# A hybrid decoder block on one Trainium2 core: the recurrence's gates from one operand of high and low rows, both gates in its columns

## The chip, the core and the metric

The kernel runs on one core of a Trainium2 chip. The time is device microseconds of an execution, and the number to compare is the median of three runs. Everything is float32 outside; inside, products on TensorE take operands of type fp32r, and each float32 operand is split into a high part (what fp32r keeps) and a low part (the rest), so that one exact product becomes three: high by high, low by high, high by low.

## The reference

The block is one layer with 512 positions and a width of 1024:

- `h = RMSNorm(x)`, `z = h @ W_in`, whose columns feed three mixers and their gates: a gated MLP with a causal matrix over chunks of 128, sparse attention (compressed, selected and window branches), and a recurrent block.
- `x = x + RMSNorm(W_o(sum of sigmoid(gate) * (branch @ W_br)))`, then `x = x + RMSNorm(SwiGLU(RMSNorm(x)))`.

The change is in the recurrent block. It has 16 heads of 64 channels:

```python
xc = causal depthwise convolution of width 4 over xr, plus conv_b
xh = xc.reshape(B, S, RNN_HEADS, RNN_HEAD_DIM)
r = sigmoid(einsum('bshi,hio->bsho', xh, w_a) + b_a)      # one 64x64 matrix per head
i = sigmoid(einsum('bshi,hio->bsho', xh, w_x) + b_x)      # another one per head
a = exp(-8 * r * softplus(-lam))
h_t = a_t * h_{t-1} + sqrt(1 - a_t**2) * (i * xc)_t
```

and its output is `h * gelu(gate)`.

## The kernel before, in words

**Layout.** Channels lie on the 128 partitions and the 512 positions along the free dimension, so a tile of 128 x 512 holds two heads of the recurrence. A product of a 128-column weight tile with a 128 x 512 operand fills one PSUM bank. A matrix of 1024 input channels takes 8 x 3 = 24 such products (function `passes`, line 259). There are eight banks: six with the tag `mm`, two with the tag `tr` in this phase.

**Stages.** First come the value half of the gated MLP (`v_half`, line 614, 96 products for each of its two halves, into four banks each, by chunk of 128 positions) and one tile for the compressed attention; then the eight tiles of the recurrence (`xr_tile`), in two batches of four, with the eight gelu tiles of its gate (`rg_tile`) and the attention's compression (`compress`, line 771) among and behind them; then the branch products, the attention, the output projection and the feed-forward network.

**A tile of the recurrence** (`xr_tile`, lines 476 to 506). 24 products give the tile; ScalarE takes it out of PSUM with scale and bias (line 488), VectorE adds the three shifted terms of the convolution (line 490). ScalarE copies the high part `ch`, VectorE subtracts for the low part `cl` (`split`, lines 131 and 136). For each of the two gates, three products (line 498) of a 128 x 128 weight tile, which has the two heads' 64 x 64 matrices on its diagonal and zeros beside them, go into a bank `tr`: high weights by `ch`, high weights by `cl`, low weights by `ch`. Sigmoid (line 500) and Tanh (line 503, the second sigmoid as `(1 + tanh)/2`) take the banks out, and one step of VectorE (line 504) multiplies by the convolved input. `yield 4` says that the gates are issued four steps after the split, behind the next tile's products.

**Behind a batch** (`rec_batch`): Tanh on each tile, one Sqrt over the four, Exp on each, two steps of VectorE and the scan per tile. Sqrt and Exp each load a table on ScalarE.

**The gate weights** (`load_wab`, lines 453 to 463). One DMA from SP (line 455) brings the array `wab`, 128 x (2 gates x 8 tiles x 128 columns), 1 MB, 8 KB per partition, with the zeros already in it. Four splits of 512 elements per partition make the high and low weights.

**Weights in general.** `unit` hands out a matrix's high and low weights; `wload` loads the raw tile (line 204; two buffers) and splits it, so that the split for the matrix after the next one is written when a matrix begins. ScalarE writes the high part, VectorE the low one.

**Start.** Eleven float32 products of ones with ones (line 349, 128 x 128 each, in one bank) run while the first loads are under way. POOL fills constants meanwhile.

**What sets the order.** The text of the kernel gives each instruction a place: `run` interleaves a main list of generators with a side list, at a given rate, and holds back a generator that yields a number. The framework then plans the order of each engine's queue from the expected times of all instructions when the kernel is built, by readiness and place in the text; `issue_after` adds a fixed order where the text wants one. On the chip every engine's queue runs strictly in the planned order. A DMA is issued by the queue of the engine named (SP, ScalarE or POOL). Tiles of one tag share their buffers in turn: the tag `row` has six, which hold `xc`, `ch`, `cl` and the gelu's temporaries; the tag `s1`, into which the raw gate weights go, has one that nothing used before.

Of the kernel before, what the change touches and what calls it, by code (L numbers as in the profile page):

```python
# [25 lines left out]
F32R = mybir.dt.float32r  # L26
I32 = mybir.dt.int32
AF = mybir.ActivationFunctionType
# [5 lines left out]
NK = 8  # L34
# [9 lines left out]
V_CW, V_CB, V_BA, V_BX, V_LAM = 48, 80, 88, 96, 104  # L44
# [8 lines left out]
def hybrid_block(ctx: ExitStack, tc: tile.TileContext, A, out):  # L53
    nc = tc.nc
    V, SC, GP, PE, SY = nc.vector, nc.scalar, nc.gpsimd, nc.tensor, nc.sync
# [42 lines left out]
    def nm(s):  # L98
        cnt[0] += 1
        return f"{s}_{cnt[0]}"  # L100

    def slab(name, dt=F32, tag=None, shape=(4, S), first=0):
        pool, bufs = (merge if tag == "m" else big, TAGS[tag]) if tag in TAGS else phase_pool[tag]
        if tag not in ("y", "mo", "f", "wab"):
            return pool.tile([128, *shape], dt, tag=tag, name=nm(name), bufs=bufs)
        size = 2064 if tag == "f" else 2112
        t = pool.tile([128, size], dt, tag=tag, name=nm(name), bufs=bufs)[:, first:first + math.prod(shape)]
        return t if len(shape) == 1 else t.rearrange(
            "p (a b) -> p a b" if len(shape) == 2 else "p (a b c) -> p a b c", **dict(zip("abc", shape)))

    def row(name, dt=F32, tag="row", first=0):
        bufs = {"row": 6, "q32": 2, "tg": 2}[tag]
        return mid.tile([128, S if tag == "row" else S + 32], dt, tag=tag, name=nm(name), bufs=bufs)[:, first:first + S]

    def bank(tag):
        return psum[1].tile([128, S], F32, tag=tag, name=nm(tag), bufs=psum[2][tag])
# [10 lines left out]
    def f32(ap):  # L127
        return ap.bitcast(F32)

    def split(src, hi, lo, lo_eng=None):  # L130
        res["hi"] = SC.activation(hi, src, AF.Copy)  # L131
        e = lo_eng or V
        if e is GP:
            GP.tensor_sub(lo, src, f32(hi))
        else:
            res["lo"] = V.tensor_sub(lo, src, f32(hi))  # L136

    res = {}
# [126 lines left out]
    def matrix(ps, xh, xl, m=128):  # L265
        hi, lo = unit()
        yield from passes(ps, hi, lo, xh, xl, m)
# [5 lines left out]
    def const0(shape, name):  # L273
        return phase_pool["s0"][0].tile(shape, F32, name=name, bufs=1)
# [7 lines left out]
    vec = const0([128, NVEC], "vec")  # L282
    SY.dma_start(vec, A["vec"])
    wload(1)
    ones = const0([128, 128], "ones")
    half = const0([128, 3, 8], "half")
# [57 lines left out]
                      start=True, stop=True)  # L344


    pw = bank("mm")
    for _ in range(11):
        PE.matmul(pw[:, :128], ones, ones, start=True, stop=True)

    gh, gl = Pair("gxh", F32R, "y"), Pair("gxl", F32R, "y")
    hh, hl = Pair("hh", F32R, "h"), Pair("hl", F32R, "h")

    def scaled(k):
# [94 lines left out]
    wab = {}  # L451

    def load_wab():
        raw = slab("wabr", tag="s1", shape=(2, NK, 128))
        SY.dma_start(raw, A["wab"])
        hi = slab("wabh", F32R, "wab", (2, NK, 128), 48)
        lo = slab("wabl", F32R, "wab", (2, NK, 128), 48)
        wab["hi"], wab["lo"] = hi, lo
        for _ in range(4):
            yield  # L460
        for k in range(0, NK, 2):
            split(raw[:, :, k:k + 2], hi[:, :, k:k + 2], lo[:, :, k:k + 2])
            yield

    yc = {}
    rec = {}
# [11 lines left out]
    def xr_tile(b, c):  # L478
        if c == 0:
            rec[b] = dict(R=slab("r", tag="y" if b else "m"), GG=slab("gg", tag="m"), TI=slab("ti", tag=("s0", "s1")[b]))  # L480
        k = 4 * b + c
        ps = bank("mm")
        yield from matrix(ps, hh, hl)
        xc = row("xc")

        def cw(w):
            return vec[:, V_CW + 8 * w + k:V_CW + 8 * w + k + 1]
        res["xc"] = SC.activation(xc, ps, AF.Identity, scale=cw(3), bias=vec[:, V_CB + k:V_CB + k + 1])
        for i in (1, 2, 3):
            res["cv"] = V.scalar_tensor_tensor(xc[:, i:], ps[:, :S - i], cw(3 - i), xc[:, i:], op0=OP.mult, op1=OP.add)  # L490
        yield
        ch, cl = row("ch", F32R), row("cl", F32R)
        split(xc, ch, cl)
        yield 4
        for g, dst in ((0, "R"), (1, "TI")):
            pg = bank("tr")
            for t, (w, x) in enumerate((("hi", ch), ("hi", cl), ("lo", ch))):
                PE.matmul(pg, wab[w][:, g, k, :], x, start=(t == 0), stop=(t == 2))  # L498
            if g == 0:
                SC.activation(rec[b]["R"][:, c, :], pg, AF.Sigmoid, bias=vec[:, V_BA + k:V_BA + k + 1])  # L500
            else:
                ti = rec[b]["TI"][:, c, :]
                last = SC.activation(ti, pg, AF.Tanh, scale=0.5, bias=half[:, 0, k:k + 1])
                res["ti"] = last, V.scalar_tensor_tensor(ti, ti, 1.0, xc, op0=OP.add, op1=OP.mult)
            yield

# [1540 lines left out]
    def xr_tiles(b, nxt):  # L2047

        tiles = four(xr_tile, b) + [nxt]
        return tiles[:1] + [behind(t, "xc", "cv") for t in tiles[1:]]  # L2050
# [4 lines left out]
    def branch(b, y, j0=0, j1=8):  # L2055
# [3 lines left out]
        return r  # L2059

    run([v_half(0), v_half(1), cmp_tile(0)], seq(norm(), load_wab()))
    run(xr_tiles(0, gate_tile()))
    tiles = xr_tiles(1, rg_tile(1, 0))
# [139 lines left out]
```

## Time and profile before

| | |
|---|---|
| median of three runs | 1093.67 us (1092.62 to 1093.85) |
| profiled execution, first to last instruction | 1090.5 us |
| mean granted clock of TensorE in it | 0.998 of full |
| TensorE busy | 1080.7 us (99%) |
| VectorE busy | 883.2 us (81%) |
| ScalarE busy | 658.9 us (60%) |
| POOL busy | 30.2 us (3%) |
| moved by DMA | 115.06 MB in 34943 packets, 3440 of them under 512 B |

The profile shows one execution. Its own total is known only as the span from the first to the last instruction; what lies around it is not in the trace. "PE" is TensorE, "PEld" its weight loads, "DVE" VectorE, "ACT" ScalarE, "SPq" and "ACTq" the queues of SP and ScalarE where they issue DMAs. A row of the timeline has the start, the duration, the engine, the line, the operation, what is written from what, the shape, how many, and in brackets the idle time before it and what ended it. A row of a group has the shortest, median and longest duration in ns, then the first and last start. A row of stretches has the stretch, its length, and for each engine the busy time and count.

### The profile page before, as it was taken

The page shows a single profiled execution, that of the slowest core. Times are in us where ns is not written, and L with a number is a line of the kernel's source. Part 1 is how long each engine was busy: PE and PEld are TensorE (multiplying, and loading weights), DVE is VectorE, ACT ScalarE, POOL GpSimd, SP SyncE. Part 2 cuts the span into 40 slices and gives each one's busy share as a digit, 9 for nine tenths or more (in the row PEclk, how much of TensorE's full clock was granted, in tenths as well). Part 3 has the DMA queues.
Part 4 walks back from the last instruction along what each step waited for, and adds up shares of the span by engine and source line. Part 5 has one row for each costly group of instructions (what it writes and reads, how often), then busy time and mean ns, then how long its engine had stood idle before and what let it go on. Part 6 is the DMA issues. An engine that isn't in the chain of part 4 may idle for free.

```text
span 1090.5 us, 16726 instructions
## 1 busy us (share of the span) xinstructions
PE 1080.7 (99%) x6440; PEld 948.2 (87%) x6440; DVE 883.2 (81%) x1552; ACT 658.9 (60%) x1207; POOL 30.2 (3%) x43
## 2 busy tenths in 40 slices
PE   9999999999999999999999999999999999999997
PEld 7888888999889888898888789988999999998885
DVE  6967779669675899998998887877987888889665
ACT  6757574454444676876777655555656665667552
POOL 1000000000000000000000000000000000022200
PEclk9999999999999999999999999999999999999999
DMA  8332325420322211102111134261323232379902
GB/s 313 104 103 84 97 85 199 182 99 20 116 78 78 78 59 39 59 20 78 59 39 59 58 119 134 76 251 39 117 78 117 100 117 94 135 213 219 185 21 96
DMA packets 34943, 115.06 MB, mean 106 GB/s; under 512 B 3440, under 2 KB 3728, under 8 KB 33968
## 3 DMA queue, kind: packets, MB, share of 16 engines
q1 hardware_dynamic: 28064, 96.93, 26.0%
q0 software_dynamic: 5216, 11.18, 5.1%
q10 hardware_dynamic: 1584, 5.90, 1.4%
q8 instruction: 50, 0.82, 0.3%
q14 instruction: 29, 0.24, 0.1%
HBM read 111.89 MB, written 2.10 MB: 105 GB/s over the span
## 4 chain that ended last, share of the span: by engine, by line
PE 96%; DVE 2%; DMA 1%; ACT 1%; issue 0%; SPq 0%; DVEq 0%; ACTq 0%
PE mm L259 37%; PE mm L1740 16%; PE mm L1876 7%; PE mm L1260 7%; PE mm L1496 4%; PE o L979 4%; PE mm L614 4%; PE sc L941 3%; PE tr L966 3%; PE tr L1876 3%; PE mm L857 2%; PE tr L771 1%; PE tr L498 1%; PE mm L1598 1%; DMA raw<-in_w_v 1%; PE tr L674 1%
## 5 line engine op out<-in xcount | busy, mean ns | idle before, releaser
L259 PE MATMUL mm<-hh,hi 128*128 128x512 f32 x504 | 199.5, 396 | 0.0
L259 PE MATMUL mm<-hh,lo 128*128 128x512 f32 x504 | 197.4, 392 | 0.0
L259 PE MATMUL mm<-hl,hi 128*128 128x512 f32 x504 | 197.0, 391 | 0.0
L136 DVE TENSOR_TENSOR lo<-raw,hi 128x1024 fp32r<-128x1024 f32 (+1 forms) x104 | 121.1, 1164 | 36.9 <-ACT hi L131 34.0
L131 ACT ACTIVATE hi<-raw 128x1024 fp32r<-128x1024 f32 (+1 forms) x104 | 105.2, 1011 | 50.3 <-PE mm L259 18.9
L259 PEld LDWEIGHTS mm<-hh,lo 128*128 128x128 f32 x504 | 94.6, 188 | 19.6
L259 PEld LDWEIGHTS mm<-hl,hi 128*128 128x128 f32 x504 | 94.7, 188 | 18.4 <-issue 0.2
L259 PEld LDWEIGHTS mm<-hh,hi 128*128 128x128 f32 x504 | 94.7, 188 | 18.1 <-PE mm L1260 0.2
L947 ACT ACTIVATE P<-P,ast 128x128 f32<-128x128 f32 (+3 forms) x128 | 70.7, 555 | 23.0 <-DVE ast L945 22.2
L945 DVE CUSTOM_DVE_ANT_0 P<-sc,mask 128x128 f32<-128x128 f32 (+3 forms) x128 | 57.9, 484 | 8.1 <-PE sc L941 7.3
L131 ACT ACTIVATE ph<-tr 128x512 fp32r<-128x512 f32 x80 | 46.9, 592 | 26.2 <-PE tr L966 23.0
L136 DVE TENSOR_TENSOR pl<-tr,ph 128x512 fp32r<-128x512 f32 x80 | 54.4, 686 | 2.9 <-ACT ph L131 0.9
L941 PE MATMUL sc<-K,q 128*128 128x512 f32 (+2 forms) x192 | 51.0, 368 | 0.0
L1740 PE MATMUL mm<-t,hi 128*128 128x256 f32 x288 | 50.7, 276 | 0.0
L1876 PE MATMUL mm<-hi,u 128*128 128x512 f32 x160 | 50.4, 390 | 0.1
L966 PE MATMUL tr<-ident,P 128*128 128x128 f32 x320 | 48.7, 273 | 0.0
L966 PEld LDWEIGHTS tr<-ident,P 128*128 128x128 f32 x320 | 39.1, 140 | 9.6 <-DVE pl L136 1.0
L136 DVE TENSOR_TENSOR lo<-bs,hi 128x1024 fp32r<-128x1024 f32 x28 | 34.1, 1222 | 13.6 <-ACT hi L131 13.5
L1740 PEld LDWEIGHTS mm<-t,hi 128*128 128x128 f32 x288 | 43.3, 188 | 0.0
L1740 PE MATMUL mm<-fh,hi 128*128 128x256 f32 x144 | 40.0, 278 | 0.0
L1740 PE MATMUL mm<-fh,lo 128*128 128x256 f32 x144 | 39.8, 276 | 0.0
L1740 PE MATMUL mm<-fl,hi 128*128 128x256 f32 x144 | 39.8, 276 | 0.0
(474 smaller groups left out, 2895.0 us busy)
## 6 DMA issues: line engine op xcount, KB each, us to landing
raw<-in_w_in SPq DMA_DIRECT2D x64, 512.0 KB, 3.5
rawp<-in_w_fi SPq DMA_DIRECT2D x20, 1024.0 KB, 4.8
bs<-in_w_fo POOLq DMA_DIRECT2D x20, 512.0 KB, 7.4
raw<-in_w_br SPq DMA_DIRECT2D x14, 512.0 KB, 3.5
w<-in_cw ACTq DMA_DIRECT2D x4, 1024.0 KB, 7.3
raw<-in_w_o SPq DMA_DIRECT2D x8, 512.0 KB, 3.9
bs<-in_w_fo SPq DMA_DIRECT2D x8, 512.0 KB, 7.9
raw<-in_w_v SPq DMA_DIRECT2D x7, 512.0 KB, 5.1
```

The costliest lines, as they stand in the source:

```text
L131: res["hi"] = SC.activation(hi, src, AF.Copy)
L136: res["lo"] = V.tensor_sub(lo, src, f32(hi))
L259: res["mm"] = PE.matmul(ps[:m, n0:n1], w[:, k * 128:k * 128 + m], x[k][:, n0:n1], start=(t == 0), stop=(t == 3 * NK - 1))
L614: res["mm"] = PE.matmul(b[c], x[k][:, c * 128:(c + 1) * 128], w[:, kk * 512:kk * 512 + 512], start=(k == 0 and t == 0), stop=(k == NK - 1 ...
L941: PE.matmul(ps[:, :w * n].rearrange("p (b n) -> p b n", b=w), lhs, K[:, i, brs[0]:brs[-1] + 1, :n], start=(i == 0), stop=(i == 1))
L945: V.tensor_tensor_reduce(out=t, in0=ps[:, b * n:b * n + n], in1=mask[0][:, S - n:], scale=-0.125, scalar=3.0e38, op0=OP.add, op1=OP.min, a ...
L947: SC.activation(t, t, AF.Exp, scale=-1.0, bias=st[:, 0, j, b:b + 1], accum_out=st[:, 1, j, b:b + 1])
L966: PE.transpose(pt[:, j * 128:(j + 1) * 128], self.part(j, br)[:, kt * 128:(kt + 1) * 128], ident)
L979: PE.matmul(po, VV[:, kt, g % 2, br].rearrange("p i d -> p (i d)"), x, start=(br == 0 and kt == 0 and t == 0), stop=(br == 1 and kt == a a ...
L1260: res["mm"] = PE.matmul(ps, u[:, k * 128:k * 128 + 128], v[:, k], start=(start and k == t == 0), stop=(k == 3 and t == 2), skip_group_chec ...
L1740: res["mm"] = PE.matmul(ps, w[:, k * 128:k * 128 + 128], x[:, k], start=(start and k == t == 0), stop=(k == 3 and t == 2), skip_group_chec ...
L1876: PE.matmul(ps, a, b, start=id(ps) not in begun, stop=i == len(ops) - 1, skip_group_check=True)
```

## The change

Per tile and head there is one operand of 128 rows: 64 rows of the head's high part in the head's own half of the partitions, and 64 rows of its low part in the other half. The weight tile for that head has the head's matrices laid twice down the rows, so that the product adds what the high and the low rows give; its first 64 columns are the first gate's matrix, its last 64 columns the second's. Two products per head (high weights, low weights) replace three per gate. The result of one head holds the first gate in the bank's lower 64 partitions and the second in the upper ones, so Sigmoid and Tanh are issued per head, on 64 partitions each, and write the head's half of the partitions. The high part is copied in two halves, and the low part is subtracted in two halves that are written across to the other half of the partitions.

The weights come in eight DMAs of 64 partitions x 8 tiles x 64 columns, four from SP and four from ScalarE, in runs of 64 elements (256 B). The splits run over the flat array, 512 elements at a time.

The warm-up has seven of the eleven products, and then six products of 64 rows, 128 columns and 512 moving elements on a tile of ones that POOL writes, alternating between the lower and the upper 64 rows and between two banks. That tile is the last of the `gxh` tiles, which the kernel fills with data later.

```diff
-    pw = bank("mm")
-    for _ in range(11):
-        PE.matmul(pw[:, :128], ones, ones, start=True, stop=True)
     gh, gl = Pair("gxh", F32R, "y"), Pair("gxl", F32R, "y")
+    GP.memset(f32(gh[7]), 1.0)
+    pw = [bank("mm") for _ in range(2)]
+    for _ in range(7):
+        PE.matmul(pw[0][:, :128], ones, ones, start=True, stop=True)
+    for _ in range(3):
+        for i in range(2):
+            r = slice(64 * i, 64 * i + 64)
+            PE.matmul(pw[i], gh[7][r, :128], gh[7][r], start=True, stop=True)
...
         raw = slab("wabr", tag="s1", shape=(2, NK, 128))
-        SY.dma_start(raw, A["wab"])
+        for n in range(2):
+            o = slice(64 * n, 64 * n + 64)
+            for i in range(2):
+                for d in range(2):
+                    (SY, SC)[d].dma_start(raw[64 * d:64 * d + 64, n, :, 64 * i:64 * i + 64], A["wab"][o, i, :, o])
...
-        for k in range(0, NK, 2):
-            split(raw[:, :, k:k + 2], hi[:, :, k:k + 2], lo[:, :, k:k + 2])
+        flat = [t.rearrange("p n k m -> p (n k m)") for t in (raw, hi, lo)]
+        for k in range(0, 2 * NK, 4):
+            split(*(t[:, k * 128:k * 128 + 512] for t in flat))
             yield
...
-        ch, cl = row("ch", F32R), row("cl", F32R)
-        split(xc, ch, cl)
+        x = [row("ch", F32R) for _ in range(2)]
+        ends = slice(0, 64), slice(64, 128)
+        for n in range(2):
+            SC.activation(x[n][ends[n]], xc[ends[n]], AF.Copy)
+        for n in range(2):
+            res["lo"] = V.tensor_sub(x[n][ends[1 - n]], xc[ends[n]], f32(x[n][ends[n]]))
         yield 4
-        for g, dst in ((0, "R"), (1, "TI")):
+        R, ti = (rec[b][n][:, c, :] for n in ("R", "TI"))
+        for n in range(2):
             pg = bank("tr")
-            for t, (w, x) in enumerate((("hi", ch), ("hi", cl), ("lo", ch))):
-                PE.matmul(pg, wab[w][:, g, k, :], x, start=(t == 0), stop=(t == 2))
-            if g == 0:
-                SC.activation(rec[b]["R"][:, c, :], pg, AF.Sigmoid, bias=vec[:, V_BA + k:V_BA + k + 1])
-            else:
-                ti = rec[b]["TI"][:, c, :]
-                last = SC.activation(ti, pg, AF.Tanh, scale=0.5, bias=half[:, 0, k:k + 1])
+            for t, w in enumerate(("hi", "lo")):
+                PE.matmul(pg, wab[w][:, n, k, :], x[n], start=(t == 0), stop=(t == 1))
+            own = ends[n]
+            SC.activation(R[own], pg[:64], AF.Sigmoid, bias=vec[own, V_BA + k:V_BA + k + 1])
+            last = SC.activation(ti[own], pg[64:], AF.Tanh, scale=0.5, bias=half[own, 0, k:k + 1])
+            if n:
                 res["ti"] = last, V.scalar_tensor_tensor(ti, ti, 1.0, xc, op0=OP.add, op1=OP.mult)
             yield
```

## The prediction

> **What bounds the kernel now.** I read the page's totals first, then the chain of work that ended last, then the list of who waited for whom, all for the kernel before.
>
> ```profile
> PE 1080.7 (99%) x6440; PEld 948.2 (87%) x6440; DVE 883.2 (81%) x1552; ACT 658.9 (60%) x1207; POOL 30.2 (3%) x43
> ...
> PE 96%; DVE 2%; DMA 1%; ACT 1%; issue 0%; SPq 0%; DVEq 0%; ACTq 0%
> ...
> PE mm L614 <- ACT hi L131: 0.6, 1, 0.6
> PE mm L614 <- ACT gxh L358: 0.6, 1, 0.6
> PE o L979 <- DVE yb L987: 0.2, 1, 0.2
> ...
> 67.84 1.36 PE tr L498 x6
> ...
> 76.00 5.44 PE mm L259 x24
> ```
>
> TensorE is busy 99% of the span and is 96% of the chain; past its first 12.2 us it waits for nothing longer than 0.2 us. A product less is therefore worth its pitch, if the engines that feed TensorE keep up. The pitch is 5.44 / 24 = 0.227 us (a single product's 0.39 us overlaps its neighbours), and the recurrence's gates cost the same: 1.36 / 6 = 0.227.
>
> **The gate products: the gain.** The products of line 498 are these groups:
>
> ```profile
> L498 PE MATMUL tr<-ch,wabh x16: 389/389/496, 67.7 to 144.5; 128*128 128x512 f32 x16
> ...
> L498 PE MATMUL tr<-cl,wabh x16: 389/389/393, 67.9 to 146.3; 128*128 128x512 f32 x16
> ...
> L498 PE MATMUL tr<-ch,wabl x16: 389/389/395, 68.1 to 146.6; 128*128 128x512 f32 x16
> ```
>
> 48 products, six in each of eight tiles. The new form takes two per head, four per tile, still 128 rows, 128 columns and 512 moving elements: 32. So 16 x 0.227 = **3.63 us** leave TensorE. The low-times-low term comes with the two products at no price.
>
> **What the gates add on ScalarE and VectorE.** Each gate now sits in half the partitions, so Sigmoid and Tanh are issued twice on 64 partitions; the high part is copied twice and the low part subtracted twice. Does half the partitions halve the time?
>
> ```profile
> 86.47 0.60 ACT L705 ACTIVATE gsig<-mm 64x512 f32<-64x512 f32 x1 [0.97 <-PE mm L701]
> 86.97 1.05 ACT L131 ACTIVATE hi<-raw 128x1024 fp32r<-128x1024 f32 x1
> ...
> L706 DVE TENSOR_TENSOR gsig<-gsig,mm x1: 681/681/681, 87.1 to 87.1; 64x512 f32<-64x512 f32 x1
> ...
> 76.31 0.68 ACT L500 ACTIVATE r<-tr,vec 128x512 f32<-128x512 f32 x1
> 76.88 0.68 ACT L503 ACTIVATE ti<-tr,half 128x512 f32<-128x512 f32 x1
> 77.45 0.73 ACT L512 ACTIVATE t<-r,sp 128x512 f32<-128x512 f32 x1
> ```
>
> No: 64x512 took 0.60 us on ScalarE (next start 0.50 later) and 0.68 on VectorE, as 128x512 does. From start to start, Sigmoid and Tanh take 0.57 each. A tile adds 0.57 + 0.57 + 0.50 = 1.64 us to ScalarE and about 0.60 to VectorE: 13.1 and 4.8 us over eight tiles, all off the chain if there is room. The two stretches in which the gates lie, and the one behind:
>
> ```profile
> 62.00:92.00 30.00, 30.00 (x135) 24.62 (x134) 19.77 (x27) 19.82 (x28) 0.00 (x0) 1.00 0.32 104
> 121.00:149.00 28.00, 28.00 (x125) 23.03 (x124) 18.98 (x25) 18.24 (x26) 0.00 (x0) 1.00 0.24 75
> ...
> 154.00:182.00 28.00, 28.00 (x130) 23.37 (x130) 26.96 (x38) 17.59 (x29) 0.00 (x0) 1.00 0.43 151
> ...
> 180.65 1.22 DVE L753 TENSOR_TENSOR xcmp<-xcmp,cpe 128x1024 f32<-128x1024 f32 x1
> ...
> 182.58 1.95 PE L771 MATMUL tr<-xcmp,w 128*128 128x124 f32 x16
> ```
>
> The columns after the length are TensorE, weight loads, VectorE and ScalarE. Four tiles shorten a stretch by 8 x 0.227 = 1.8 us and add 6.6 to ScalarE: 26.4 of 28.2 us (94%) and 24.8 of 26.2 (95%); VectorE reaches 22.2 and 21.4. It fits, with little left. TensorE has other tiles' products and six banks to run ahead on, and weights are split two units ahead. The place where lateness shows is the end of a batch: the last tile's second Sigmoid and Tanh stand ahead of the batch's Tanh, Sqrt and Exp, so that chain moves up by 3.63 - 1.14 = 2.5 us where TensorE moves up by 3.63. Behind it VectorE is full (26.96 of 28 us) until it finishes the operand of the first compression at 181.87, read at 182.58: 0.71 us to spare. Late by 1.14 - 0.71 = 0.43. Bounds: 0, if the next tile's products are put ahead of the compression, and 1.14, if the spare is gone already. I take **0.5 us** lost.
>
> **The weights' load.** One load of 1 MB becomes eight, four each from SP and ScalarE, in runs of 256 B: 4096 runs.
>
> ```profile
> L455 SPq DMA_DIRECT2D wabr<-in_wab x1: 544/544/544, 22.3 to 22.3; - x1
> ...
> DMA to landing us min/median/max: 6.2/6.2/6.2
> ...
> L759 POOL DMA_DIRECT2D cw<-in_cw x2: 535/624/713, 2.1 to 200.8; - x2
> ...
> DMA to landing us min/median/max: 2.0/4.2/6.4
> ...
> out<-yo SPq DMA_DIRECT2D x1, 128.0 KB, 1.9
> ...
> 16.00:20.00 4.00, 4.00 (x19) 3.33 (x18) 1.56 (x5) 2.66 (x5) 0.00 (x0) 1.00 1.02 403
> ...
> 27.43 2.55 SPq L204 DMA_DIRECT2D raw<-in_w_v  x2
> ...
> 28.88 2.17 ACT L131 ACTIVATE wabh<-wabr 128x512 fp32r<-128x512 f32 x4
> 31.00 0.72 ACT L447 ACTIVATE gs<-gs,rmul 128x512 f32<-128x512 f32 x1
> ...
> 32.36 0.68 DVE L448 SCALAR_TENSOR_TENSOR vt<-gs,mm 128x512 f32<-128x512 f32 x1
> ...
> 33.67 0.40 PE L614 MATMUL mm<-hi,gxh 128*128 128x512 f32 x1
> ...
> 40.50 1.06 ACT L131 ACTIVATE hi<-raw 128x1024 fp32r<-128x1024 f32 x1 [1.28 <-PE mm L614]
> ```
>
> It landed at 22.3 + 6.2 = 28.5, and its four splits were put at 28.88. The price of short runs is not in the trace for this size. Lower bound: no later, the bytes being the same. Upper: the small load of line 759, 256 runs of 256 B, landed in 2.0 us at best; were all of that the runs' own time, 16 times as many would take 32. A store of 128 KB, twice the bytes in long rows, took 1.9 us too, so most of the 2.0 is latency, and I take 3 us more, landing near 31.5 (an estimate; any landing before about 60 still serves the first gates at 67.7). The Trainium skill, "DMA: Bandwidth & Descriptors" (Specifications, and Rules for kernel authors), speaks against this edit: runs under 512 B miss line rate, and splitting over partition halves or queues gains nothing, as they share the same engines. At half of the 403 GB/s that the engines moved from 16 to 20 us, 1 MB would take 2.6 us longer by that rule.
>
> What stands behind the splits on ScalarE is the Tanh at 31.00, then VectorE's step at 32.36, which frees the bank that TensorE fills at 33.67: 0.6 us to spare. The order on each engine is planned ahead from expected times (these splits ran before work written earlier). If the plan expects the load late, the splits go into later gaps of ScalarE, such as the 1.28 us before 40.50, and cost **0**; that is my value. If it does not, that is the third rival. The four splits themselves keep 512 elements. On SP four issues of about 0.5 us end near 24.5, before its next load at 27.43, which shares the engines with what is left of the runs; its weights are used from about 39.4 us on (12.17 + 120 products x 0.227), so a few microseconds of that are hidden. ScalarE's four issues go beside its running work, as the compression's weight loads do:
>
> ```profile
> 160.75 0.72 ACT L519 ACTIVATE r<-r,spm 128x512 f32<-128x512 f32 x1
> 161.14 0.34 ACTq L745 DMA_DIRECT2D w<-in_cw  x1
> 161.36 0.63 ACT L447 ACTIVATE gs<-gs 128x512 f32<-128x512 f32 x1
> ```
>
> **The warm-up.** 22 passes (two for each of eleven products) become 14, and six products of 64 rows by 512 elements on a tile that POOL fills.
>
> ```profile
> 1.12 4.07 PE L349 MATMUL mm<-ones 128*128 128x128 f32 x22 [1.12 <-DVE warm L293]
> 5.79 1.20 PE L614 MATMUL mm<-hi,gxh 128*128 128x512 f32 x4 [0.59 <-ACT gxh L358]
> ...
> 12.17 1.20 PE L614 MATMUL mm<-hi,gxh 128*128 128x512 f32 x4 [0.61 <-ACT hi L131]
> ...
> 1.71 0.31 POOL L693 MEMSET kcb<- 128x256 f32 x1
> ```
>
> 14 passes at 4.07 / 22 = 0.185 us end near 3.7; POOL's fill, twice the 0.31 us of half the size and from 1.71 on, is done by 2.4. Six at 0.227 end at 5.1, before the first real product, which waits for ScalarE until 5.79. Were they twice as slow, 6.4: 0.6 late, and the 0.61 us that TensorE waits for weights before 12.17 takes that up. Value **0**. Bounds: 0 (no gain: both waits end with loads) and, should the 24 real products before 12.17 run at half pace, 24 x 0.227 - 0.61 = 4.8 us.
>
> **Sum.** 1090.5 - 3.63 + 0.5 = 1087.4 us of span. The median of the runs, 1093.67, lies 3.2 above the profiled span of 1090.5; with the same 3.2 the time is **1090.5 us**, 0.29% faster. By 0.2% (2.2 us) a gain can just be told from none.
>
> **Rivals.**
> 1. *ScalarE becomes the bound of the gates' stretches*. For: 94 and 95% full, and the gaps that it has today end with products of TensorE and convolutions of VectorE, so not each can be filled. If 87% is all that it reaches, 26.4 us need 30.3 and 24.8 need 28.5: both stretches last as long as before, and the products saved turn into waits. Against: TensorE can run ahead and ScalarE has room afterwards. Half to nothing of the gain is left: 1092 to 1094, centre 1093.
> 2. *The order falls better*: a new plan removes the small waits of two engines as well, a microsecond or two: 1088.5. Nothing in the profile promises it.
> 3. *Slower: ScalarE stands before the late weights.* The splits stay near 28.88 and the load lands later. Of each microsecond beyond 0.6, TensorE loses all at 33.67. Landing at 32.6 eats the 3.1 us gained; from there on it is slower. Landing at 35 costs 6.1 - 0.6 = 5.5, less 3.1: 1096. For: 4096 short runs, and the weights of the next units are loaded at the same time. Against: the gaps after 36 us are free to take them, and need is at 67.7.
>
> **How the numbers follow.** Forecast 46% (own range 1089.7 to 1091.4), rival 1 22%, rival 2 8%, rival 3 24% (3 points of it the warm-up's bad end, which costs about the same). Faster by more than 0.2%: 45 + 8 + 2 of rival 1 = 55%. Within: 1 + 18 + 4 of rival 3 = 23%. Slower: 20 + 2 = 22%. The range 1088.8 to 1095.8 leaves out some 6% below and 12% above.
>
> **What would show it.** Line 498's successor with 32 products; TensorE's starts behind them 0.45 us earlier with each tile, 1.8 after the fourth, 3.6 after the eighth, and no idle on it. Rival 1 would show as idle of TensorE on ScalarE or VectorE between 62 and 150 us; the 0.5 us as a wait on line 753's operand near 179; rival 3 as a wait on line 614 near 33 us with ScalarE waiting for the weights' load; the warm-up as a first real product after 5.8 or a wider pitch after it. A shift that appears at the gates and is gone later would prove the sum wrong though its terms hold.

## The result, and the profile after

The changed kernel takes 1100.49 us (median, 1099.92 to 1101.2) against 1093.76 beside it (1092.62 to 1093.91): a ratio of **1.0064** with an interval of 1.005 to 1.0079, 6.7 us slower. Forecast were 1090.5 us and a range up to 1095.8. The profiled execution has a span of 1098.2 us where the kernel before had 1090.5.

The totals of the page after (busy time, share of the span, instructions):

```profile
PE 1081.6 (98%) x6422; PEld 946.1 (86%) x6422; DVE 891.0 (81%) x1560; ACT 677.3 (62%) x1231; POOL 30.7 (3%) x44
```

TensorE has 18 instructions less (16 gate products and two of the warm-up) and is busy a microsecond longer, in a span that is 7.7 us longer. So products became slower somewhere, and TensorE waits. The list of its waits in the changed kernel (total, times, longest):

```profile
PE mm L626 <- ACT gxh L361: 3.3, 1, 3.3
PE tr L511 <- DVE ch L505: 2.6, 3, 1.1
...
PE mm L259 <- DVE lo L136: 1.1, 1, 1.1
PE tr L723 <- ACT gsig L719: 0.6, 1, 0.6
```

None of these four was there before, where the first products waited twice for 0.6 us and later ones never for more than 0.2. One stands at the start, three in the gates' stretches. Line 626 is the old 614, line 511 the old 498, line 505 the new low subtraction.

**The start.** TensorE's timeline in the changed kernel (start, duration, then what is written from what):

```profile
4.40 1.25 PE L355 MATMUL mm<-gxh 64*128 64x512 f32 x6
8.99 2.07 PE L626 MATMUL mm<-hi,gxh 128*128 128x512 f32 x4 [3.35 <-ACT gxh L361]
10.87 1.55 PE L626 MATMUL mm<-hi,gxl 128*128 128x512 f32 x4
12.26 1.09 PE L626 MATMUL mm<-lo,gxh 128*128 128x512 f32 x4
```

The new warm-up is over at 5.65, half a microsecond behind the 5.1 that was reckoned and still ahead of 5.79, but the first real product starts at 8.99 instead of 5.79. The first four then take 10.87 - 8.99 = 1.88 us, 0.47 each, twice the pitch of 0.227; full pace returns near 12. The windows of the same execution (length, then busy time and count of TensorE, weight loads, VectorE, ScalarE and POOL, then the granted clock) agree:

```profile
8.00:9.00 1.00, 0.01 (x1) 0.01 (x1) 0.73 (x3) 1.00 (x4) 0.00 (x0) 0.72 1.09 436
9.00:10.00 1.00, 1.00 (x2) 0.82 (x3) 1.00 (x2) 0.56 (x1) 0.00 (x0) 0.50 1.00 384
...
11.00:12.00 1.00, 1.00 (x4) 0.79 (x3) 0.55 (x1) 1.00 (x3) 0.00 (x0) 0.57 1.06 259
12.00:16.00 4.00, 4.00 (x19) 3.27 (x18) 3.33 (x5) 1.88 (x4) 0.00 (x0) 1.00 1.09 356
```

The 17th real product starts at 14.10 where it started at 9.59 before: 4.5 us late. A microsecond of that is won back, since the small waits of before (0.61 at 12.17) now vanish behind the lateness; where the compressed attention's tile begins, at 51.36 us before and 54.92 after, the two kernels stand 3.6 us apart.

The Trainium skill, "TensorE: Matmul & The Clock Gate" (What's actually happening), says that the clock falls to half after an idle window of about 3.4 us and needs as long to return. The trace agrees in size: 3.35 us idle, a clock of 0.50, full again some 3 us after the first product. In c_warm_only (below) the pace is half behind only 2.4 us of idle, which that sentence alone does not cover.

**The gates.** ScalarE and VectorE around one tile of the changed kernel:

```profile
79.44 0.67 ACT L513 ACTIVATE r<-tr,vec 64x512 f32<-64x512 f32 x1
80.13 0.69 ACT L514 ACTIVATE ti<-tr,half 64x512 f32<-64x512 f32 x1
80.84 0.68 ACT L513 ACTIVATE r<-tr,vec 64x512 f32<-64x512 f32 x1
81.55 0.68 ACT L514 ACTIVATE ti<-tr,half 64x512 f32<-64x512 f32 x1
82.25 1.06 ACT L131 ACTIVATE hi<-raw 128x1024 fp32r<-128x1024 f32 x1
83.22 1.27 ACT L503 ACTIVATE ch<-xc 64x512 fp32r<-64x512 f32 x2
84.52 1.33 ACT L524 ACTIVATE t<-r,sp 128x512 f32<-128x512 f32 x2
```

```profile
83.35 1.23 DVE L136 TENSOR_TENSOR lo<-raw,hi 128x1024 fp32r<-128x1024 f32 x1 [0.40 <-ACT hi L131]
84.61 1.40 DVE L505 TENSOR_TENSOR ch<-xc,ch 64x512 fp32r<-64x512 f32 x2
```

No row of ScalarE has idle time in brackets: its queue is full. Sigmoid and Tanh of the two heads take 82.25 - 79.44 = 2.81 us, where two on 128 partitions took 77.45 - 76.31 = 1.14; the two high copies take 1.30, where one took about 0.6. That is 2.4 us more per tile, where the prediction had 1.64. The high copy waits its turn until 83.22, the low subtraction stands on VectorE behind the subtraction for the next weights, and TensorE waits for it, in the gate products that follow:

```profile
85.44 0.47 PE L511 MATMUL tr<-ch,wabh 128*128 128x512 f32 x1 [1.03 <-DVE ch L505]
85.75 0.40 PE L511 MATMUL tr<-ch,wabl 128*128 128x512 f32 x1
86.16 0.47 PE L511 MATMUL tr<-ch,wabh 128*128 128x512 f32 x1
86.47 0.40 PE L511 MATMUL tr<-ch,wabl 128*128 128x512 f32 x1
```

These start 0.31, 0.41 and 0.31 us apart, not 0.227: the second head's low part comes some 0.7 us behind the first's (1.40 us for the two). Windows around this place, first of the kernel before, then of the changed one:

```profile
76.00:92.00 16.00, 16.00 (x74) 13.01 (x73) 11.14 (x16) 10.73 (x17) 0.00 (x0) 1.00 0.29 97
```

```profile
76.00:94.00 18.00, 16.86 (x73) 13.04 (x71) 14.69 (x20) 17.58 (x26) 0.00 (x0) 1.00 0.25 76
...
132.00:154.00 22.00, 20.42 (x86) 15.48 (x85) 17.00 (x22) 21.29 (x29) 0.00 (x0) 1.00 0.27 76
```

ScalarE was busy 10.73 of 16 us; now it is busy 17.58 of 18 and, in the second batch, 21.29 of 22. From the starts of TensorE's products between 60 and 155 us I summed what each took beyond a pitch of 0.227: 0.29 us before, 7.02 after. Less the 3.63 saved, the gates' stretches cost 7.02 - 0.29 - 3.63 = **3.1 us** net in this execution. With the 3.6 of the start that makes 6.7. The first compression product on the late operand (line 771, now 783), at 182.58 before, comes at 189.25, 6.7 later.

The middle part hardly varies from one execution to another. From the start of the compressed attention's tile to the first compression product, the five profiles with the whole of the new gates (this one and, below, a_all_sp, d_gates_only, j_fill_vector and l_fill_sp) are 3.09 to 3.16 us longer than the kernel before, and the four whose edits lie elsewhere (b_load_only, c_warm_only, i_memset_vector, m_load_sp) differ from it by 0.02 at most.

Another 1.0 us is added between there and the end of the span, with no single wait above 0.3 us. This need not be the change's: i_memset_vector, whose edit ends at the start, is 1.4 us longer there too, and the profile of the kernel before, with a span of 1090.5, is one of its faster executions (its executions beside the experiments have 1090.0 to 1095.1).

### The profile page after: what moved, and what is told of

Read it like the earlier page. It is cut to its first block, busy times and chain, and to the rows that moved or that the text cites. A ratio compares the mean times of both kernels' runs of the same rounds, so it can differ in the third digit from the quotient of the medians.

```text
span 1098.2 us, 16756 instructions
## 1 busy us (share of the span) xinstructions
PE 1081.6 (98%) x6422; PEld 946.1 (86%) x6422; DVE 891.0 (81%) x1560; ACT 677.3 (62%) x1231; POOL 30.7 (3%) x44
## 4 chain that ended last, share of the span: by engine, by line
PE 82%; DVE 2%; ACT 1%; issue 0%; DMA 0%; DVEq 0%; ACTq 0%
PE mm L259 29%; PE mm L1752 15%; PE mm L1272 7%; PE mm L1888 6%; PE mm L1508 4%; PE o L991 4%; PE sc L953 3%; PE tr L978 3%; PE tr L1888 3%; PE mm L869 2%; PE tr L783 1%; PE mm L1610 1%; PE tr L686 1%; DVE lo L136 1%; PE tr L891 1%
```

## The experiments

All ratios are to the kernel before, run beside the kernel in question. Four kernels first took the change apart.

**a_all_sp: the changed kernel with all eight loads on SP.**

```diff
-                    (SY, SC)[d].dma_start(raw[64 * d:...], A["wab"][o, i, :, o])
+                    SY.dma_start(raw[64 * d:...], A["wab"][o, i, :, o])
```

> The changed kernel with all eight weight loads issued from SP. Theory H (the four loads on ScalarE's queue were issued from 1.3 us on, among the first loads, and cost 3.6 us at the start): the first real product starts near 5.8 us again, the granted clock stays full, and the time falls from 1100.5 to 1097 us. Theory W (the new warm-up products let the clock fall): unchanged, 1100.5. Theory B (the 256-byte runs cost wherever they are issued): the stall moves to the queue of splits near 33 us, 1099 to 1102.

Measured: 1101.6 us, 1.0068 (1.0051 to 1.0085). The first real product starts at 9.42, and TensorE again waits 3.4 us for `gxh`. The loads left the start (SP issues them from 21.9 us on) and nothing came back. So ScalarE's loads alone are not what delays the start.

**b_load_only: the kernel before with eight loads.**

```diff
-        SY.dma_start(raw, A["wab"])
+        for n in range(2):
+            for i in range(2):
+                for d in range(2):
+                    p, m = slice(64 * d, 64 * d + 64), slice(64 * i, 64 * i + 64)
+                    (SY, SC)[d].dma_start(raw[p, n, :, m], A["wab"][p, n, :, m])
```

> The kernel before with its gate weights loaded by eight loads of 64 partitions in 256-byte runs, alternately from SP and ScalarE, to the old places; gates and warm-up as before. Theory H: first real product 3 us late and the clock at half for some us after it, 1093.8 + 3.6 = 1097.4. Theory W: 1093.8. Theory B: 1094 to 1097, with the stall near 33 us instead of the start.

Measured: 1097.86 us, 1.0033 (1.002 to 1.0045): 4.4 us between the medians for the load alone, 3.6 by the ratio. First two of TensorE's waits, then SP's timeline, then one of SP's waits:

```profile
PE mm L618 <- ACT hi L131: 2.7, 2, 1.5
PE tr L343 <- DVE rstd L322: 1.9, 1, 1.9
```

```profile
13.32 0.33 SPq L204 DMA_DIRECT2D raw<-in_w_v  x1
21.47 0.33 SPq L375 DMA_DIRECT2D xrow<-in_x  x1
```

```profile
SPq L375 <- DMA wabr<-in_wab: 7.8, 1, 7.8
```

ScalarE's queue issues its four loads early (1.33, 9.74 and from 15.72 us), in the middle of the first loads of data. SP's second `xrow` load, at 13.78 before, stands 7.8 us for one of them and leaves at 21.47 (the transfer issued at 9.74 landed 11.7 us later, at 21.45); the norm's factors (`rstd`) and the next weights come late, and TensorE waits for both. Why a load on SP waits for one that ScalarE issued, the trace doesn't tell; the releaser is inferred.

**c_warm_only: the kernel before with the new warm-up** (the warm-up's part of the diff above, nothing else).

> The kernel before with only the new warm-up products. Theory H: the warm-up ends before the first real product, 1093.8 +- 0.5. Theory W: the clock falls to half after it, 1095 to 1097.

Measured: 1096.92 us, 1.0029 (1.0017 to 1.0041): 3.5 us for the warm-up alone, which the prediction had at nothing. ScalarE's timeline, first before and then here:

```profile
4.49 0.63 ACT L131 ACTIVATE hi<-raw 128x512 fp32r<-128x512 f32 x1 [1.74 <-DMA raw<-in_w_v]
5.03 0.71 ACT L358 ACTIVATE gxh<-xt,vec 128x512 fp32r<-128x512 f32 x1
...
5.74 0.71 ACT L358 ACTIVATE gxh<-xt,vec 128x512 fp32r<-128x512 f32 x1
...
7.10 0.63 ACT L131 ACTIVATE hi<-raw 128x512 fp32r<-128x512 f32 x1 [0.56 <-DMA raw<-in_w_v]
```

```profile
4.81 0.63 ACT L131 ACTIVATE hi<-raw 128x512 fp32r<-128x512 f32 x1 [2.06 <-DMA raw<-in_w_v]
...
7.13 0.63 ACT L131 ACTIVATE hi<-raw 128x512 fp32r<-128x512 f32 x1 [1.35 <-DMA raw<-in_w_v]
7.67 1.32 ACT L361 ACTIVATE gxh<-xt,vec 128x512 fp32r<-128x512 f32 x2
```

The order on ScalarE is another one: the two `gxh` activations, whose data are there, now stand behind the second `hi` copy, whose data land at 7.1. TensorE has nothing to do from 6.05 to 8.42, and its next 12 products run at half pace until 13.7:

```profile
4.41 1.65 PE L355 MATMUL mm<-gxh 64*128 64x512 f32 x6
8.42 2.08 PE L617 MATMUL mm<-hi,gxh 128*128 128x512 f32 x4 [2.37 <-ACT gxh L361]
```

Whether the idle time brought the half pace back is not shown. The six warm-up products start in three pairs; here the last pair starts 0.43 us behind the one before, in the changed kernel (1.25 us for the six) 0.25. So here the full pace may not have come yet when the warm-up ended.

**d_gates_only: the new gates with the old warm-up and one load** (the new weight layout comes ready in `wab`).

> The kernel before with only the new gates: the weights are laid out in HBM in the new form and come in one load from SP as before; old warm-up. Theory G (the doubled half-partition operations fill ScalarE and VectorE, TensorE waits in the gates' stretches): 1093.8 + 3.3 = 1097.1, TensorE waiting on the low subtraction. Rival P (the late start had upset the planned order, the gates themselves gain): 1093.8 - 3.1 = 1090.7 with no wait of TensorE in the gates.

Measured: 1097.2 us, 1.0033 (1.0023 to 1.0044). The start is as before; the waits of the gates' stretches are those of the changed kernel (2.5 us in three for the low subtraction, 1.0 for the weights' low part, 0.7 for `gsig`). So the gates, which were to win 3.1 us, lose 3.8 by themselves. The parts alone add to 3.5 + 4.4 + 3.8 = 11.7 us, all together cost 6.7 (by the ratios 10.4 and 7.0): the warm-up and the load both delay the same start, and the lateness of the one covers that of the other.

Four more looked for the cause within each part.

**i_memset_vector: c_warm_only with the ones laid by VectorE.**

```diff
-    GP.memset(f32(gh[7]), 1.0)
+    V.memset(f32(gh[7]), 1.0)
```

> The kernel before with the changed kernel's warm-up (7 products of ones and 6 of 64 rows by 512 columns), where the ones in gxh are laid by VectorE instead of GpSimd; nothing else. With GpSimd's fill (the run of the warm-up alone) the planned ScalarE order had both gxh activations behind the second hi copy, the first real product started at 8.42 us instead of 5.79 and the clock was half for some 5 us: 1096.9. Theory O (the order is the cause, and the new products by themselves cost nothing): with VectorE's fill the planned order is again hi, gxh, lt, gxh, lt, hi, the first real product starts at 5.8 to 6.2 us and the time is that of before, 1093.0 to 1094.2. Rival W (the new products themselves hold TensorE or fail to warm its clock): the first real product is late or slow whatever ScalarE's order, 1096 to 1097.

Measured: 1093.5 us, 1.0001 (0.9992 to 1.001). ScalarE's and TensorE's timelines:

```profile
5.46 0.71 ACT L361 ACTIVATE gxh<-xt,vec 128x512 fp32r<-128x512 f32 x1
...
6.18 0.71 ACT L361 ACTIVATE gxh<-xt,vec 128x512 fp32r<-128x512 f32 x1
...
7.17 0.64 ACT L131 ACTIVATE hi<-raw 128x512 fp32r<-128x512 f32 x1 [0.19 <-DMA raw<-in_w_v]
```

```profile
6.22 1.21 PE L617 MATMUL mm<-hi,gxh 128*128 128x512 f32 x4 [0.34 <-ACT gxh L361]
7.27 1.07 PE L617 MATMUL mm<-hi,gxl 128*128 128x512 f32 x4
```

The same products, the same bytes, the fill on another engine: the old order is back, and so is the time. In this order the new warm-up costs nothing; the order that the plan fell into with GpSimd's fill costs 3.5 us. On the chip that fill was over by 2.3 us, long before anything needed it, so it moved the plan and not the work. Why the plan turns is not settled.

**e_two_acts: d_gates_only with one Sigmoid and one Tanh per tile.**

```diff
-            SC.activation(R[own], pg[:64], AF.Sigmoid, bias=vec[own, V_BA + k:V_BA + k + 1])
-            last = SC.activation(ti[own], pg[64:], AF.Tanh, scale=0.5, bias=half[own, 0, k:k + 1])
+            if n == 0:
+                SC.activation(R, pg, AF.Sigmoid, bias=vec[:, V_BA + k:V_BA + k + 1])
+            else:
+                last = SC.activation(ti, pg, AF.Tanh, scale=0.5, bias=half[:, 0, k:k + 1])
```

> The run of the gates alone (new operands, 4 products per tile, weights laid in the new form, old warm-up and one load), but with one Sigmoid over all 128 partitions of the first bank and one Tanh over all 128 of the second, in place of two of each over 64 partitions. It leaves out half of the gates' Sigmoids and Tanhs and takes the values of the other gate for a half, so the gates' values are not the reference's; counts of the other instructions are the same. Gates alone: 1097.2. Theory G1 (ScalarE's four half activations, 0.70 us apart for 2.8 us per tile against 1.25 before, are what the products wait for): time falls by 3 to 6 us to 1091 to 1094, and the waits of the gate products on the low subtraction and of L259 on lo go. Rival G2 (the split high copies and low subtractions, or the products' own semaphores, are the cost): the time stays at 1096 to 1097.5 and the waits stay.

Measured: 1091.34 us, 0.9979 (0.997 to 0.9989). With 1.67 us per tile off ScalarE, the 32 products run at their pitch and the waits on the low part are gone; of the 3.63 us, 2.1 arrive; where the other 1.5 went stays open. The windows of one stretch, of the kernel before, of d_gates_only and of e_two_acts (after the length TensorE, weight loads, VectorE, ScalarE):

```profile
60.00:92.00 32.00, 32.00 (x144) 26.29 (x143) 20.71 (x28) 19.82 (x28) 0.00 (x0) 1.00 0.30 98
```

```profile
60.00:92.00 32.00, 30.29 (x132) 23.82 (x131) 23.84 (x32) 25.80 (x36) 0.00 (x0) 1.00 0.28 83
```

```profile
60.00:92.00 32.00, 31.81 (x142) 25.71 (x141) 23.99 (x33) 23.69 (x33) 0.00 (x0) 1.00 0.30 99
```

The split copies and subtractions are in both of the last two; only Sigmoid and Tanh differ. TensorE loses 1.71 us of this stretch in the one and 0.19 in the other.

**g_acts_split: the kernel before with Sigmoid and Tanh in halves.**

```diff
-                SC.activation(rec[b]["R"][:, c, :], pg, AF.Sigmoid, bias=vec[:, V_BA + k:V_BA + k + 1])
+                for o in ends:
+                    SC.activation(rec[b]["R"][o, c, :], pg[o], AF.Sigmoid, bias=vec[o, V_BA + k:V_BA + k + 1])
```

and the same for Tanh.

> The kernel before with its six products per tile, but Sigmoid and Tanh each issued in two halves of 64 partitions (rows 0 to 63, then 64 to 127), so 4 activations per tile. Theory G1 (ScalarE's half activations alone): ScalarE gets 1.2 to 1.55 us per tile more and the time rises by 2 to 5 us: 1095.5 to 1098.5, with TensorE waits behind ScalarE or the low parts between 62 and 150 us. Rival G2 (they have room on ScalarE; the cost is in the operand's split or in the products): 1093 to 1094.5.

Measured: 1094.71 us, 1.001 (1.0001 to 1.002): 1.2 us, between the two expectations. Doubling Sigmoid and Tanh is nearly free while the operand is made by one copy and one subtraction and the products run longer. The profile has 0.8 us of it as a wait at the compression's second operand. So the added work does most of its harm together: the halved activations alone cost 1.2 us, the split copies and subtractions alone (e_two_acts) at most the 1.5 that did not arrive, both 3.63 + 3.8 = 7.4, on a queue that then has no gap left.

**k_copies_pool: d_gates_only with the high copies on GpSimd.**

```diff
-            SC.activation(x[n][ends[n]], xc[ends[n]], AF.Copy)
+            GP.tensor_copy(x[n][ends[n]], xc[ends[n]])
```

> The gates alone (1097.2) with the two high copies per tile on GpSimd in place of ScalarE: ScalarE loses 1.27 us per tile, GpSimd, idle in these stretches, gets two copies of 64 by 512 (the nearest rows: its 128x512 fill took 0.53 us, its 128x512 select 0.65). Theory G1 (ScalarE's time is the bound): 1091 to 1094.5, the idle of TensorE on the low subtraction mostly gone. Rival: the copies on GpSimd are long (over 1.3 us each) or hold VectorE up, and the low subtraction is later still: 1098 to 1105.

Measured: 1096.95 us, 1.0034 (1.0021 to 1.0048), as d_gates_only and as neither theory had it. GpSimd's row and VectorE's beside it:

```profile
84.55 1.63 POOL L496 CAST ch<-xc 64x512 fp32r<-64x512 f32 x2 [4.90 <-ACT ti L507]
```

```profile
84.57 1.13 DVE L509 SCALAR_TENSOR_TENSOR ti<-ti,xc 128x512 f32<-128x512 f32 x1 [0.18 <-ACT ti L507]
85.73 1.70 DVE L498 TENSOR_TENSOR ch<-xc,ch 64x512 fp32r<-64x512 f32 x2
```

A copy takes 0.82 us there, and VectorE's step beside it 1.13 instead of 0.69. ScalarE had gaps again, but the chain from `xc` to the low part was no shorter.

The next four joined the pieces and tried the last engine.

**m_load_sp: b_load_only with all eight loads on SP** (`SY` in place of `(SY, SC)[d]`).

> The kernel before with the weights loaded by eight transfers as in the changed kernel, but all eight issued by SP (old layout, old gates, old warm-up). With four of them on ScalarE's queue (the run of the load alone, 1097.9) the first left at 1.33 us, ScalarE's first activation came at 5.57, and SP's second xrow load stood 7.8 us for a transfer of wabr, so that TensorE waited 4.6 us for hi and for rstd. Theory Q (the ScalarE queue's issues, early and in SP's way, are the load's cost): the first real product is at 5.8 to 6.1 us, xrow's second load near 13.8, and the time 1093.0 to 1094.5. Rival S (eight short-run transfers cost by themselves, whoever issues them): 1095.5 to 1098.

Measured: 1094.29 us, 1.001 (0.9998 to 1.0021). SP's second `xrow` load leaves at 12.43, and TensorE waits neither for `hi` nor for `rstd`:

```profile
12.43 0.43 SPq L375 DMA_DIRECT2D xrow<-in_x  x1
```

Eight transfers in runs of 256 B cost 2.3 us at the most, and perhaps nothing. The rest of b_load_only's loss, 3.4 us by the medians and 2.5 by the ratios, is the price of putting four of them on ScalarE's queue.

**j_fill_vector: the changed kernel with VectorE's fill** (the edit of i_memset_vector).

> The whole changed kernel with one difference: the ones for the warm-up are laid by VectorE instead of GpSimd, which in the kernel before brought the warm-up's 3.4 us back. Theory: the planned ScalarE order at the start becomes that of the load alone (gxh, hi, gxh, hi), so the clock does not fall, but the loads on ScalarE's queue and the gates still cost: 1093.5 + 4.4 (load alone) + 3.8 (gates alone) = 1101.7 if the parts add; 1099 to 1102.5. Rival: without the warm-up's loss 3.4 us of the change's 6.7 come back and the time is 1096.5 to 1098.

Measured: 1099.6 us, 1.0059 (1.0041 to 1.0077). Less than a microsecond comes back, since the load's delay, until now covered, shows: the first real product starts at 7.14, SP's `xrow` load waits 7.0 us for a transfer of `wabr`, and TensorE 1.0 for `rstd`. Its first eight real products take 0.43 us each.

**l_fill_sp: the changed kernel with VectorE's fill and all loads on SP.**

> The whole changed kernel with VectorE laying the ones and all eight loads on SP. Theory (three causes: the warm-up's order, the ScalarE queue's loads, the gates' halves): only the gates' loss is left, 1096.3 to 1098.3, and the first real product starts at 5.8 to 6.3 us with the clock at 1.00. Rival (the eight transfers cost by themselves): 1099 to 1101.

Measured: 1096.84 us, 1.0031 (1.002 to 1.0042): with both causes of the start away, what is left is what d_gates_only costs. By the ratios, a_all_sp and j_fill_vector, which each took one of the two away, won half a microsecond at most; taking both wins 3.6 us (1.0064 less 1.0031).

**n_copy_vec: d_gates_only with the second head's high copy on VectorE.**

```diff
-            SC.activation(x[n][ends[n]], xc[ends[n]], AF.Copy)
+            if n:
+                V.tensor_copy(x[n][ends[n]], xc[ends[n]])
+            else:
+                SC.activation(x[n][ends[n]], xc[ends[n]], AF.Copy)
```

> The gates alone (1097.2) with the second head's high copy on VectorE and the first head's on ScalarE: ScalarE loses 0.65 us per tile, VectorE gets one copy of 64 by 512 (the nearest rows: its subtraction of that size takes 0.70). With both copies on GpSimd, where each took 0.82 and stretched VectorE's operations beside it (0.69 to 1.13), nothing was won, so the chain xc, high copy, low subtraction counts and not ScalarE's sum alone. Theory C (the chain's length behind ScalarE's queue): the first copies of the two heads run beside each other, the low parts come some 0.6 us sooner, and the time falls by 1 to 4 us to 1093.5 to 1096.2. Rival V (VectorE has no room: 22 to 24 of 30 us busy): 1096.5 to 1099.

Measured: 1095.32 us, 1.0016 (1.0006 to 1.0026), some 1.9 us better than d_gates_only. The copy is cheap on VectorE:

```profile
79.05 0.42 DVE L497 CAST ch<-xc 64x512 fp32r<-64x512 f32 x1
```

The Trainium skill, "VectorE: DVE Perf Modes" (The perf-mode tier table), has float32 copies in SBUF at twice the rate of an operation on two tensors, and the rows agree in kind: 0.42 against 0.70 us for the subtraction of the same size.

**o_copies_vec: both high copies on VectorE.**

> The gates alone (1097.2; with one head's copy on VectorE 1095.3) with both high copies on VectorE, where a cast of 64 by 512 took 0.42 us in the run with one. ScalarE loses 1.27 us per tile, VectorE gets 0.84, and the planned order of VectorE then has the two casts and two low subtractions in one stretch of 2.2 us, before the next weights' subtraction instead of behind it in five tiles. Theory C (the chain from xc to the low parts is what the gate products wait for): their waits on the low parts go, and the time falls to 1090.5 to 1094. Rival S (ScalarE's and VectorE's sum: VectorE is then busy 25 to 28 of 30 us): the wait moves to L259 on the weights' lo, and the time is 1094 to 1097.

Measured: 1096.08 us, 1.0027 (1.0018 to 1.0036). The waits of the gate products shrink to one of 0.6 us, as theory C has it, and yet the time does not fall: 1.0027 against 1.0016 with one copy moved, intervals that overlap. VectorE's and TensorE's timelines, later on:

```profile
182.42 1.23 DVE L758 TENSOR_TENSOR x<-xcmp,cpe 128x1024 f32<-128x1024 f32 x1
```

```profile
183.75 2.02 PE L776 MATMUL tr<-x,w 128*128 128x124 f32 x16 [1.71 <-issue]
```

The first of the compression's two operands (line 753 before, ready at 178.5) is ready at 183.65, and the compression, which TensorE reached at 181.9, starts 0.1 us after that; the trace names no releaser for this wait, and the operand is the one that fits. The prediction had placed a wait at the second of these operands: it comes, at the first, as soon as VectorE bears the copies.

**p_repaired: the changed kernel with VectorE's fill, all loads on SP and both copies on VectorE.**

> The whole changed kernel with the three causes taken away as far as they can be: ones laid by VectorE, eight loads on SP, both high copies on VectorE. If the three causes are the whole loss, it is within 1 us of the run with the gates alone and both copies on VectorE: 1090.5 to 1095, at best faster than before by up to 0.25 %. If something else costs, it stays at 1096 or more.

Measured: 1096.06 us, 1.0026 (1.0017 to 1.0035), the time of o_copies_vec, as the first sign of the expectation asks, though also the "1096 or more" of the second: o_copies_vec itself had turned out at 1096.08, so the two signs no longer exclude each other. Against o_copies_vec nothing else in the change costs, within a microsecond; what remains is the gates'. No version of the new gates that computes the reference beat the kernel before: three engines were tried for the copies, and with each the waits cost more than the products saved. Only e_two_acts, which computes other gates, was faster.

## Why the prediction was wrong, point by point

- **"The warm-up: value 0"** failed, and by 3.5 us. Of its own terms the fill's time held; the passes were mis-sized by 0.8 us, harmlessly. The mean of 0.185 us per pass mixed two paces (before, the first 13 passes start some 0.21 apart, the last nine 0.11), and the fourteen took 3.35 us, not 2.6, all at the slow one; the warm-up ended at 5.65 to 6.06 instead of 5.1. The step that failed is another: it took for granted that the first real product "waits for ScalarE until 5.79". The order on ScalarE was planned anew when the ones were laid by GpSimd, and the activation for that product went behind a copy that waits for a DMA (c_warm_only, i_memset_vector). The bad end that it named, 24 real products at half pace for 4.8 us, had the right size by luck: most of the loss is a first product 2.6 to 3.2 us late behind a changed order, with 7 to 12 products at half pace after it. How far a warm-up too weak has a part in that pace stays open: with the old order back and almost no gap, the same warm-up was followed by full pace in i_memset_vector and by half pace in l_fill_sp.
- **The load, "cost 0"** failed, by 4.4 us alone (3.6 by the ratio). Three of its sentences held or nearly so: the last load landed at 32.96, forecast near 31.5 (5.5 us from issue in the median, 8.6 the longest); the splits went into later gaps (30.04 and 36.97); nothing was lost near 33.67. SP's own four issues did not end near 24.5: two of them stood behind its next load, until 28.95. What failed is "ScalarE's four issues go beside its running work": they were reckoned near 22 us, where SP's load stood, but ScalarE's queue reached them at 1.32, 5.58, 7.53 and 16.34, among the first loads of data, and SP stood for one of them (b_load_only, m_load_sp). In the whole change this was covered by the warm-up's delay (a_all_sp, j_fill_vector, l_fill_sp). Rival 3, slower by the load, had the sign and 1096, but its place and mechanism did not occur. The 2.6 us longer transfer that the prediction set beside its own 3 assumed half the pace for short runs, which is a choice of the prediction; no run isolates the transfer, and on the kernel's time m_load_sp has 1.1 us, with nothing to 2.3 in its interval.
- **3.63 us from 16 products** held: 32 products remain, 16 with the high weights and 16 with the low ones, at the old pitch where nothing made them wait (e_two_acts).
- **ScalarE's 1.64 us per tile** was mis-sized: 2.4. The 0.57 us from one activation to the next was measured on 128 partitions, and 0.50 behind an activation of 64 partitions that a full one followed; halves that alternate start 0.70 apart. VectorE's 0.60 was 0.7.
- **"It fits, with little left", 0.5 us lost** failed: the gates lose 3.8 us instead of winning 3.1. The fill of 94% was an average over 30 us. Within the stretch the work has its order and its due times: from 76 to 94 us ScalarE is at 98%, what stands first is served first, and the high copy that the gate products need comes late. Of the rivals, the first named this: ScalarE the bound, and the products saved turning into waits, as idle of TensorE between 62 and 150 us. Its price stopped at "both stretches last as long as before"; nothing stops a full engine there, and they lasted 3 us longer.
- **The place of the loss**, the compression's operand, shows in o_copies_vec, where VectorE bears the copies, and in g_acts_split; it was wrong for this kernel, where the loss came before it.
- **What would show it** worked: the first real product after 5.8 and the wider pitch behind it pointed to the warm-up, the idle on VectorE's low part between 62 and 150 us to the gates.

## What to carry to other kernels

Where an order is planned for all engines together, an edit is not only its instructions: a constant laid by an idle engine, or a load given to a second queue, can move work that nobody touched, so read the queue's order before costing an edit at nothing. Products saved on TensorE are worth their pitch only if the engines that feed it have room for the work that replaces them: count that work in the stretch itself, at the spacing that the new shapes have, not as a share of a longer time. And where two delays lie at one place, taking either away shows little; take both away, or put each alone into the kernel before.

## What the runs showed of the hardware

- Activations on 64 partitions that alternate between the halves start 0.69 to 0.71 us apart, on 128 partitions 0.57; a half one followed by a full one took 0.59 (g_acts_split, from 84.07 to 84.66). Half the partitions is not half the time, and here it is more than the whole.
- TensorE's pace at the start differs between executions with the same warm-up: in i_memset_vector it is full from 6.22 us on, in l_fill_sp, with a gap of 0.39 us ahead, the first eight products take 0.45 us each, though the six warm-up products start at the same times to 0.01 us. The Trainium skill, "TensorE: Matmul & The Clock Gate" (What's actually happening), has an activity window that runs freely, so that the turn to full pace moves from run to run; these rows fit that. The granted clock of the profile does not always show it: it was 0.50 in the changed kernel, but 1.00 in c_warm_only, where this window holds 6 products in 2 us, so the pitch of the products has to be read beside it:

```profile
9.00:11.00 2.00, 2.00 (x6) 1.59 (x5) 0.82 (x2) 0.55 (x1) 0.00 (x0) 1.00 1.05 407
```

- GpSimd copying in SBUF slows VectorE: the step of line 509 took 0.86 us in the mean of its eight and 1.13 at most in k_copies_pool, 0.69 in d_gates_only.
